# Attention with bias on one core: other engines for the first casts, another order of the first copies, one more exp bank on VectorE, other load times

## The chip, the cores and the metric

The kernel runs on one core of a Trainium2 chip. The metric is the device time of one execution in microseconds (us). The kernel before took 242.43 us (median of 3 runs, 241.94 to 243.75).

The engines are named as the profile names them: PE is TensorE (PEld its weight loads), ACT ScalarE, DVE VectorE, POOL GpSimd, SP SyncE. The last two issue most of the DMAs.

## The reference

```python
batch, n_heads, seq_len, head_dim = 4, 8, 1024, 64
scores = np.matmul(q, k.transpose(0, 1, 3, 2)) / np.sqrt(head_dim) + bias
attn = np.exp(scores - scores_max) / (np.sum(np.exp(scores - scores_max), axis=-1, keepdims=True) + 1e-8)
return np.matmul(attn, v)
```

q, k and v are float32 of shape 4 x 8 x 1024 x 64, the bias is 1 x 1 x 1024 x 1024 and the same for all 32 heads.

## The kernel before

**Pairs, passes, fills.** Two heads make a pair, so there are 16 pairs (0 to 15). The 1024 queries are cut into eight chunks of 128, and these into three passes: A (chunks 6 and 7), B (3 to 5), C (0 to 2). The pairs run in three groups: 0 to 3 through A, B, C; 4 to 8 through C, A, B; 9 to 15 through B, C, A. A step is one head of a pair in one pass. It has two fills, one of the PSUM buffer `sx` and one of `sy`, so there are 192 fills. A fill has two banks of 512 columns in pass A and three in B and C, 512 banks in all.

**Scores without reloading the bias.** Scores stay in PSUM. At a pass's start the bias is put there by matmuls (`restart` in `s_fill`, line 151). From then on each fill adds the new head's scores and subtracts the old head's in one matmul of 128 rows: the top 64 rows of KA/QA or KB/QB hold one head, the bottom 64 the other, and QA and QB carry the signs. So the next fill of a buffer waits for the exps that read it.

**Exp.** ScalarE turns the banks of a fill into weights in bf16 (`s_exp`, line 202). Of some fills the last bank is left to VectorE, which works the exp out by a polynomial in seven instructions (`d_fixed`, line 215, and the six of `d_steps`, line 220). Such a bank is called marked; a fill is marked by `mark_next` (line 586). TensorE multiplies the weights by v, with a column of ones for the sum (`av_blocks`, line 252, instruction at L265), VectorE divides (`evac`), and SP stores.

**Preparing q and k.** Loads issued by GpSimd convert to bf16 (`load_qk`, `load_v`). TensorE transposes them into the PSUM tile `px` (L140), and VectorE copies from there into KA, KB, QA, QB (`tp_done`, line 715). For pairs 0 to 3 it makes every copy itself; later, SP's DMAs make those into KB and QB.

**The prologue, lines 281 to 487, is written out by hand.** Pair 0's and pair 1's first tiles and bias chunks 6 and 7 come by SP and ScalarE queues as float32 into staging space (`sk0`, `sk0b`, `sc[6]`, `sc[7]`, `sk1`) and are cast to bf16 by ScalarE, VectorE and, for one tile, GpSimd. Seven matmuls on zeros (line 366) come first on TensorE. Then: casts of pair 0's first k, transposes (L376, L380), copies (L382 to L384), scores L393 and bias L402, the first exps (L406), cast and transposes of pair 0's second k (L428, L429, L432), its copies (L434, L435), scores of chunk 7, and so on to the first planned fill at L478.

**The rest is planned.** The loop at line 926 gives TensorE, VectorE and ScalarE their instructions in the order that a table of costs and due times makes (`EXP`, `EXP0`, `PSL`, `PSU`, `URG`, `NEAR`, `REM` and others, lines 490 to 491). Each engine then works through its own list in order. `mark_next` marks a fill when not too much of VectorE's work is still to do (`ch_left`, `REM`), and only from fill `DMIN` to fill 192 - `DTAIL`. `loads` (line 675) issues the loads of pairs 4 to 15 when so many fills have had their exps: q and k when the count is over twice the pair's first step minus `LEADK` (28), v with `LEADV` (16). Each such load waits for the exp issued last before it.

```python
            while next_load < NP and s > 2 * first_step[next_load] - LEADK and pieces[0][0] > next_load - 4:
                for x in load_qk(next_load):
                    after(x, exps[-1])
```

Of the kernel before, what the change touches and what calls it, by code (L numbers as in the profile page):

```python
# [9 lines left out]
BF = mybir.dt.bfloat16  # L10
# [6 lines left out]
def kernel(  # L17
# [202 lines left out]
    def d_steps(ch):  # L220
        y = ys[ch % 2]
        e = de.tile([P, 512], BF, name="e")
        dtiles[ch] = e
        lo = y.bitcast(U16).rearrange("p (q w) -> p q w", w=2)[:, :, 0]
        hi = y.bitcast(I16).rearrange("p (q w) -> p q w", w=2)[:, :, 1]
        v_ = nc.vector
        return [
            (350, lambda: v_.tensor_scalar(sf, lo, G / 65536.0, None, op0=ALU.mult)),  # L228
            (350, lambda: v_.tensor_scalar(sp, hi, 0.0, 128.0, op0=ALU.max, op1=ALU.mult)),  # L229
            (610, lambda: v_.scalar_tensor_tensor(sb, sf, U2, sf, op0=ALU.add, op1=ALU.mult)),  # L230
            (610, lambda: v_.scalar_tensor_tensor(y, sf, U1, sf, op0=ALU.add, op1=ALU.mult)),  # L231
            (610, lambda: v_.scalar_tensor_tensor(sb, sb, V2, sp.bitcast(BF), op0=ALU.add, op1=ALU.mult)),  # L232
            (720, lambda: v_.scalar_tensor_tensor(e[:], y, V1, sb, op0=ALU.add, op1=ALU.mult)),  # L233
        ]
# [46 lines left out]
    with tc.manual_schedule():  # L281
# [145 lines left out]
        k0b = [sk0b[:, i * 256:(i + 1) * 256].rearrange("p (c d) -> p c d", d=D) for i in range(2)]  # L427
        cast(v_, kr0[:, 1, 4:], k0b[1])  # L428
        cast(nc.scalar, kr0[:, 1, :4], k0b[0])  # L429
# [4 lines left out]
        v_.tensor_copy(KA[D:, 0, :HK], pk0f[D:, :HK])  # L434
        v_.tensor_copy(KA[D:, 0, HK:], pk0f[D:, HK:])  # L435
# [9 lines left out]
        v_.tensor_copy(btraw[:, 7, HK:], sc[7][:, HK:])  # L445
# [45 lines left out]
        DMIN, DTAIL, DMAL, RING, PSL, PSU, URG, NEAR, REM = 14, 10, 5200, 36, 100, 200, 16, 2, 4000  # L491
        LEADK, LEADV = 28, 16
# [9 lines left out]
        raw_at = {(2, 1, 0): 12500, (2, 0, 6): 12900, (3, 1, 0): 14800, (3, 0, 6): 15200, (0, 0, 0): 16300,  # L502
                  (1, 0, 0): 23000, (2, 0, 0): 24000, (3, 0, 0): 25000}
        pieces = [(2, 1, 0, 8), (2, 0, 6, 2), (3, 1, 0, 8), (3, 0, 6, 2), (0, 0, 0, 6), (1, 0, 0, 6), (2, 0, 0, 6),
# [26 lines left out]
        def fill_banks(s):  # L531

            banks = range(2) if s in pre_done else range(nbanks(steps[s // 2][0]))
            return sorted(banks, key=lambda b: read_end.get(s - 2, {}).get(b, 0)) if s - 2 in pre_slots else list(banks)
# [20 lines left out]

        def act_cost(s):
            return EXP0 * (1 if cut_of(s) is None else 2) + EXP * banks_act(s)
# [28 lines left out]
        def mark_next(s):  # L586

            nonlocal nch
            if s in pre_slots or s != len(fill_end) or not DMIN <= s < NS - DTAIL or s - 1 in mark or len(open_ch) >= 3 \
                    or len(ch_run) >= 2 or ch_left[0] > REM:  # L590
                return
            mark.add(s)
            d_of[s, nbanks(steps[s // 2][0]) - 1] = nch
            av_left[s] -= 1
            open_ch[nch] = 1
            ch_run.append(nch)
            ch_left[0] += 3850
            nch += 1
# [75 lines left out]

        def loads():

            nonlocal next_load, next_v, dma_t
            s, t = len(act_end), t_act
            while next_load < NP and s > 2 * first_step[next_load] - LEADK and pieces[0][0] > next_load - 4:
                for x in load_qk(next_load):  # L680
                    after(x, exps[-1])
                dma_t = max(dma_t, t + 2800) + 1500
                raw_at[next_load, 1, 0] = dma_t
                dma_t += 1500
                raw_at[next_load, 0, 0] = dma_t
                next_load += 1
            while next_v < NP and s > 2 * first_step[next_v] - LEADV \
                    and not any(units[u][1] == next_v - RP for u in range(av_u, NU)):
                for x in load_v(next_v):
                    after(x, exps[-1])  # L690
                dma_t = max(dma_t, t + 2800) + 2000
                v_ready[next_v] = dma_t + 1000
                next_v += 1

        def pe_piece():
# [9 lines left out]
            ready = max(free + LATE, raw_at[pr, which, c0]) + SEM  # L705
# [7 lines left out]
            return ready, cost, emit  # L713

        def tp_done(pr, which, c0, n, px, tag, t):
# [33 lines left out]
            if which:  # L749
                if pr <= 3:  # L750
                    step(c1, lambda: nc.vector.tensor_copy(KB[:D, r, cs], flat[:D]), [("KBt", pr)])
                if pr <= 2:
                    step(c1, lambda: nc.vector.tensor_copy(KB[D:, r1, cs], flat[D:]), [("KBb", pr + 1)])
                step(c1, lambda: nc.vector.tensor_copy(KA[:, r, cs], flat), [("KA", pr)], 0, free)  # L754
            else:
                if pr <= 3:
                    step(c1, lambda: nc.vector.tensor_copy(QB[:D, r, cs], flat[:D]), [("QBt", pr)])
                if pr <= 2:
                    step(c1, lambda: sc_(QB[D:, r1, cs], flat[D:], -1.0, None, op0=ALU.mult), [("QBb", pr + 1)])
                step(cq, lambda: sc_(QA[:, r, cs], flat, sgn[:, :1], None, op0=ALU.mult), [("QA", pr)], 0, free)  # L760
# [14 lines left out]

            def next_(t1):
                cost, f = todo.pop(0)

                def run(t2):
                    f(t2)  # L780
                    if todo:
                        next_(t2 + cost)
                dve_q.append((t1, 0, cost, run))
            next_(t)
# [59 lines left out]
        def pe_pick():  # L844
            s = len(fill_end)
            f = pe_fill()
            if f and f[0] <= t_pe:
# [12 lines left out]
            for kind, c in enumerate((pe_piece(), pe_pre(), pe_av())):  # L860
# [3 lines left out]
                if kind == 0 and in_a and f and f[0] <= start + 300:  # L864
# [34 lines left out]
        def act_pick():  # L899
# [20 lines left out]
            for s, a, z in todo:  # L920
                t0 = max(t, (pre_done[s] + 470 if a == 2 and s in pre_done else bank_end[s][z - 1]) + P2E)
                t = t0 + EXP0 + EXP * (z - a)
# [70 lines left out]
```

## Time and profile before

| | |
|---|---|
| runs | 241.94, 242.43, 243.75 us |
| the profiled execution | 242.75 us, span 240.8 us |
| exps of the planned part (L204) on ScalarE | 258 instructions, 125.0 + 119.4 us busy |
| banks on VectorE (L233, last step of each) | 39 |
| copies QA (L760) on VectorE | 18, 670 ns in the mean |
| v loads by GpSimd | 32, 128 KB each, 10.3 us from issue to landing (median) |
| k loads by GpSimd | 14, 256 KB each, 4.3 us |

A row of the page's groups has line, engine, operation, tile written and tile read, count, busy time, mean of one, and idle time before it. The timeline has start, length, engine, line, operation and shapes, and in brackets how long the engine was idle before and what released it. Exps that follow one another overlap in the trace by about 0.1 us, so the busy time of ScalarE counts a little more than the time that passes. TensorE's ends are modelled.

The start and the end of the planned part, in ScalarE's timeline:

```
15.26 1.02 ACT L204 ACTIVATE E<-sx 128x1024 bf16<-128x1024 f32 x1
235.91 1.08 ACT L204 ACTIVATE E<-sy 128x512 bf16<-128x512 f32 x2
```

### The profile page before, as it was taken

Reading aid. Unit: us, or ns where it says so; the run is one execution under the profiler, and the core shown is the slowest. Engines: PE = TensorE matmul, PEld = TensorE weight load, DVE = VectorE, ACT = ScalarE, POOL = GpSimd, SP = SyncE. Lnnn points to the kernel's source line nnn. Section 1 sums busy time; section 2 is a strip of 40 time slices with the busy share of each in tenths; the row PEclk is TensorE's granted clock in tenths of the full one; section 3 lists DMA queues with packets and bytes.
Section 4 is the critical chain, followed back from the end, with each engine's and each line's share of the span. In section 5 each row is a group of like instructions: output and inputs, shape, how many; then the busy total and the mean of one; then the engine's idle time right before and its main releaser. Section 6 shows DMA issues by size and latency. Waiting matters only on the chain.

```text
span 240.8 us, 9418 instructions
## 1 busy us (share of the span) xinstructions
PE 225.0 (93%) x4009; PEld 188.6 (78%) x4009; DVE 219.0 (91%) x456; ACT 226.2 (94%) x273; POOL 56.7 (24%) x80
## 2 busy tenths in 40 slices
PE   7996989999999999999999999989999899998993
PEld 3775868888877889998777787777888777797882
DVE  3576999979999999999999999979999999999992
ACT  4588999999999999999999999989999999999993
POOL 4594322255241000013365444200000000000000
PEclk9999999999999999999999999999999999999998
DMA  7899997989999522039899999994121121111112
GB/s 223 223 147 181 171 164 136 169 165 180 228 197 200 135 69 66 5 93 169 142 168 196 227 237 220 195 198 97 38 65 39 34 69 36 33 35 35 50 42 67
DMA packets 60633, 30.98 MB, mean 129 GB/s; under 512 B 36016, under 2 KB 56624, under 8 KB 60592
## 3 DMA queue, kind: packets, MB, share of 16 engines
q0 software_dynamic: 42272, 13.50, 54.2%
q1 hardware_dynamic: 18176, 16.62, 25.4%
q8 instruction: 31, 0.51, 0.9%
q10 hardware_dynamic: 144, 0.26, 0.5%
q14 instruction: 10, 0.08, 0.1%
HBM read 29.36 MB, written 8.39 MB: 157 GB/s over the span
## 4 chain that ended last, share of the span: by engine, by line
PE 57%; ACT 16%; DVE 15%; issue 7%; DMA 4%; ACTq 0%; DVEq 0%
PE po L265 18%; PE sx L176 16%; PE sy L176 15%; ACT E L204 15%; PE px L140 5%; DMA out_dram<-ob 3%; DVE scr L216 2%; DMA E<-in_k_dram 1%; DVE scr L231 1%; DVE scr L230 1%; DVE ob L277 1%; DVE QA L760 1%; DVE KA L754 1%; DVE scr L232 1%; DVE e L233 1%
## 5 line engine op out<-in xcount | busy, mean ns | idle before, releaser
L204 ACT ACTIVATE E<-sy 128x512 bf16<-128x512 f32 (+2 forms) x141 | 125.0, 941 | 0.6 <-PE sy L176 0.2
L204 ACT ACTIVATE E<-sx 128x1024 bf16<-128x1024 f32 (+2 forms) x117 | 119.4, 1049 | 3.3 <-PE sx L176 2.7
L265 PE MATMUL po<-VV,E 128*128 128x65 bf16 x1892 | 82.9, 194 | 2.3 <-DVE KA L754 0.7
L265 PEld LDWEIGHTS <-E 128*128 128x128 bf16 x1892 | 75.3, 98 | 9.9 <-issue 2.7
L176 PEld LDWEIGHTS <-KA 128*128 128x128 bf16 x648 | 47.3, 97 | 10.8 <-issue 3.1
L176 PEld LDWEIGHTS <-KB 128*128 128x128 bf16 x600 | 43.7, 98 | 13.7 <-issue 5.7
L176 PE MATMUL sx<-QB,KB 128*128 128x128 bf16 (+2 forms) x300 | 34.8, 251 | 4.8 <-ACT E L204 2.8
L176 PE MATMUL sy<-QA,KA 128*128 128x128 bf16 (+2 forms) x312 | 36.8, 251 | 0.8
L176 PE MATMUL sx<-QA,KA 128*128 128x128 bf16 (+2 forms) x312 | 35.8, 252 | 0.7 <-ACT E L204 0.2
L176 PE MATMUL sy<-QB,KB 128*128 128x128 bf16 (+2 forms) x300 | 34.9, 251 | 0.7 <-ACT E L204 0.5
L134 POOL DMA_DIRECT2D VV<-in_v_dram x32 | 28.9, 905 | 22.7 <-ACT E L204 10.8
L233 DVE SCALAR_TENSOR_TENSOR e<-scr 128x512 bf16<-128x512 f32 x39 | 26.8, 688 | 0.9
L232 DVE SCALAR_TENSOR_TENSOR scr<-scr 128x512 f32<-128x512 f32 x39 | 26.6, 683 | 0.0
L230 DVE SCALAR_TENSOR_TENSOR scr<-scr 128x512 f32<-128x512 f32 x39 | 26.6, 682 | 0.0
L231 DVE SCALAR_TENSOR_TENSOR scr<-scr 128x512 f32<-128x512 f32 x39 | 26.6, 682 | 0.0
L277 DVE TENSOR_TENSOR ob<-po,rs 128x384 f32<-128x384 f32 (+2 forms) x49 | 24.8, 506 | 1.7
L131 POOL DMA_DIRECT2D kr<-in_k_dram x12 | 8.7, 723 | 68.5 <-ACT E L204 63.9
L228 DVE TENSOR_SCALAR scr<-scr 128x512 f32<-128x512 uint16 x39 | 17.4, 447 | 0.1
L229 DVE TENSOR_SCALAR scr<-scr 128x512 int16<-128x512 int16 x39 | 17.0, 435 | 0.0
L216 DVE TENSOR_SCALAR scr<-sx 128x512 int32<-128x512 f32 x24 | 16.4, 683 | 0.2
L760 DVE TENSOR_SCALAR QA<-px,sgn 128x1024 bf16<-128x1024 bf16 (+2 forms) x18 | 12.1, 670 | 2.7 <-PE px L140 2.5
L140 PE MATMUL px<-ident,qr 128*64 128x128 bf16 x256 | 11.4, 224 | 1.1 <-issue 1.1
(81 smaller groups left out, 175.5 us busy)
## 6 DMA issues: line engine op xcount, KB each, us to landing
out_dram<-ob SPq DMA_DIRECT2D x32, 192.0 KB, 2.6
VV<-in_v_dram POOLq DMA_DIRECT2D x32, 128.0 KB, 10.3
kr<-in_k_dram POOLq DMA_DIRECT2D x14, 256.0 KB, 4.3
KB<-KA SPq DMA_DIRECT2D x24, 128.0 KB, 7.0
qr<-in_q_dram POOLq DMA_DIRECT2D x12, 256.0 KB, 6.5
QB<-qn SPq DMA_DIRECT2D x22, 128.0 KB, 7.0
out_dram<-ob SPq DMA_DIRECT2D x15, 128.0 KB, 2.3
btraw<-in_bias_dram POOLq DMA_DIRECT2D x2, 768.0 KB, 9.9
```

What stands on the lines that cost most here:

```text
L134: return [nc.gpsimd.dma_start(out=VV[:, pr % RP, t * NCH:(t + 1) * NCH, :D], in_=vf[pr][:, t].rearrange("p (c d) -> p c d", d=D)) for t in ...
L140: nc.tensor.transpose(px[t * D:(t + 1) * D, c, :], src[:, t, c0 + c, :], ident[:])
L176: m = nc.tensor.matmul(o, lhsT, rhs, start=restart and i == 0, stop=i == len(todo) - 1 or not restart, skip_group_check=True)
L204: x = nc.scalar.activation(E[:, at:at + (hi - lo) * 512], XY[s % 2][:, lo * 512:hi * 512], ACTF.Exp, scale=scale)
L216: i = nc.vector.tensor_scalar(ys[ch % 2].bitcast(I32), XY[s % 2][:, b * 512:(b + 1) * 512], scale * LOG2E * 65536.0, 127.0 * 65536.0, op0= ...
L228: (350, lambda: v_.tensor_scalar(sf, lo, G / 65536.0, None, op0=ALU.mult)),
L230: (610, lambda: v_.scalar_tensor_tensor(sb, sf, U2, sf, op0=ALU.add, op1=ALU.mult)),
L231: (610, lambda: v_.scalar_tensor_tensor(y, sf, U1, sf, op0=ALU.add, op1=ALU.mult)),
L232: (610, lambda: v_.scalar_tensor_tensor(sb, sb, V2, sp.bitcast(BF), op0=ALU.add, op1=ALU.mult)),
L233: (720, lambda: v_.scalar_tensor_tensor(e[:], y, V1, sb, op0=ALU.add, op1=ALU.mult)),
L265: nc.tensor.matmul(po[u][:, h - hs[0], c - c0, :], e_block(s, col), VV[:, pr % RP, h * NCH + kc, :], start=first, stop=left[u] == 0, skip_ ...
L277: nc.vector.tensor_tensor(ob[:], acc[:, :, :, :D], rs[:].to_broadcast([P, nh, W, D]), op=ALU.mult)
```

## The change

- **Prologue.** Eight matmuls on zeros instead of seven. Bias chunk 6's last 384 columns and chunk 7's last 512 are cast by GpSimd instead of VectorE. Pair 0's second k is cast whole by VectorE instead of by halves on VectorE and ScalarE. The copy of pair 0's second half of k stands ahead of the copy of q. Pair 3's q load stands ahead of its k load on GpSimd.
- **First copies of pairs 0 to 3.** Of a k tile, the copy into KB's top is made first; then the list waits until the first q copy of that pair is made; KA follows; the copy into the next pair's KB bottom comes last (for pairs up to 2). For q, QB's top is first, then QA, then the next pair's QB bottom. The PSUM tile is free after the last of these.
- **Loads.** A new function `gate` sets them: pairs 4 to 8 from fill 18 on, five fills apart, v twelve fills later; pairs 9 to 15 from fill 56 on, six apart, v eight later.
- **Planner.** Costs of VectorE's steps, of single-bank exps and several thresholds; marked fills are allowed up to fill 184 instead of 182. The number of banks on VectorE goes from 39 to 40.
- **Order rules.** The early fill of a pass's third bank (`pe_pre`) goes ahead of other TensorE work when it is that fill's turn; in pass A a transpose may go ahead of a fill that is up to 0.3 us away.

```diff
-            (350, lambda: v_.tensor_scalar(sf, lo, G / 65536.0, None, op0=ALU.mult)),
...
-            (720, lambda: v_.scalar_tensor_tensor(e[:], y, V1, sb, op0=ALU.add, op1=ALU.mult)),
+            (340, lambda: v_.tensor_scalar(sf, lo, G / 65536.0, None, op0=ALU.mult)),
...
+            (650, lambda: v_.scalar_tensor_tensor(e[:], y, V1, sb, op0=ALU.add, op1=ALU.mult)),
...
+        cast(g, btraw[:, 6, 5 * P:], sc[6][:, 5 * P:])
         for pr in (2, 3):
             if pr == 3:
                 cast(g, kr1[:, 1].rearrange("p c d -> p (c d)"), sk1[:, 512:])
+                load_q(pr, 6, 8)
             x = g.dma_start(out=raws[pr, 1].rearrange("p t c d -> p t (c d)"), in_=kf[pr])
             if pr == 2:
                 after(x, behind)
-            load_q(pr, 6, 8)
+            if pr == 2:
+                cast(g, btraw[:, 7, HK:], sc[7][:, HK:])
+                load_q(pr, 6, 8)
...
-        for i in range(7):
+        for i in range(8):
...
+        on(1, 2, 3, v_.tensor_copy(KA[:D, 0, HK:], pk[1][:D]))
         v_.tensor_copy(QB[:D, 0, 6 * P:], pq_[:D].rearrange("p c q -> p (c q)"))
-        on(1, 2, 3, v_.tensor_copy(KA[:D, 0, HK:], pk[1][:D]))
         nc.scalar.copy(btraw[:, 6, :5 * P], sc[6][:, :5 * P])
-        v_.tensor_copy(btraw[:, 6, 5 * P:], sc[6][:, 5 * P:])
...
-        cast(v_, kr0[:, 1, 4:], k0b[1])
-        cast(nc.scalar, kr0[:, 1, :4], k0b[0])
+        cast(v_, kr0[:, 1], sk0b.rearrange("p (c d) -> p c d", d=D))
...
-        v_.tensor_copy(btraw[:, 7, HK:], sc[7][:, HK:])
...
-        DMIN, DTAIL, DMAL, RING, PSL, PSU, URG, NEAR, REM = 14, 10, 5200, 36, 100, 200, 16, 2, 4000
-        LEADK, LEADV = 28, 16
+        DMIN, DTAIL, DMAL, RING, PSL, PSU, URG, NEAR, REM = 14, 8, 5200, 38, 60, 150, 24, 3, 5000
+        G0, G1, G2, G3, G4, G5 = 18, 5, 12, 56, 6, 8
...
+        def gate(pr, v=0):
+
+            return G0 + G1 * (pr - 4) + G2 * v if pr < 9 else G3 + G4 * (pr - 9) + G5 * v
...
-            while next_load < NP and s > 2 * first_step[next_load] - LEADK and pieces[0][0] > next_load - 4:
+            while next_load < NP and s > gate(next_load) and pieces[0][0] > next_load - 4:
...
-            while next_v < NP and s > 2 * first_step[next_v] - LEADV \
+            while next_v < NP and s > gate(next_v, 1) \
...
-            ready = max(free + LATE, raw_at[pr, which, c0]) + SEM
+            ready = max(free + (LATE if pr > 3 else 100), raw_at[pr, which, c0]) + SEM
...
             if which:
+                early = pr <= 3
+                if early:
+                    step(c1, lambda: nc.vector.tensor_copy(KB[:D, r, cs], flat[:D]), [("KBt", pr)])
+                step(c1, lambda: nc.vector.tensor_copy(KA[:, r, cs], flat), [("KA", pr)], 0, None if pr <= 2 else free)
+                if pr <= 2:
+                    step(c1, lambda: nc.vector.tensor_copy(KB[D:, r1, cs], flat[D:]), [("KBb", pr + 1)], 0, free)
+            else:
+                early = False
                 if pr <= 3:
-                    step(c1, lambda: nc.vector.tensor_copy(KB[:D, r, cs], flat[:D]), [("KBt", pr)])
+                    step(c1, lambda: nc.vector.tensor_copy(QB[:D, r, cs], flat[:D]), [("QBt", pr)], 0, lambda t2: q_first(t2))
...
+            pre = pe_pre()
+            if pre and s in pre_slots:
+                return (max(t_pe, pre[0]),) + pre[1:]
...
-                if kind == 0 and in_a and f and f[0] <= start + 300:
+                if kind == 0 and in_a and f and f[0] <= start + (300 if dist > 6 else -300):
```

More of the change, by code (lines that the diff above doesn't have):

```diff
@@ L533, in fill_banks @@
             banks = range(2) if s in pre_done else range(nbanks(steps[s // 2][0]))
-            return sorted(banks, key=lambda b: read_end.get(s - 2, {}).get(b, 0)) if s - 2 in pre_slots else list(banks)
+            return sorted(banks, key=lambda b: read_end.get(s - 2, {}).get(b, 0)) if s in pre_slots or s - 2 in pre_slots else list(banks)
         def bank_cost(s):
@@ L780, in run @@
                     f(t2)
-                    if todo:
+                    if todo and early and len(todo) == n_all - 1 and resume.get(pr) != "go":
+                        resume[pr] = next_
+                    elif todo:
                         next_(t2 + cost)
                 dve_q.append((t1, 0, cost, run))
+            n_all = len(todo)
             next_(t)
```

44 lines of the change are left out of this document (23 added, 21 removed).

## The prediction

> **What bounds the kernel now.** I read the page's busy times first, then ScalarE's timeline for its waits, then the chain of waits around the early ones, then the stretches in windows. Times are in us from the span's start.
>
> ```profile
> PE 225.0 (93%) x4009; PEld 188.6 (78%) x4009; DVE 219.0 (91%) x456; ACT 226.2 (94%) x273; POOL 56.7 (24%) x80
> ```
>
> ScalarE (ACT) is the fullest engine, with VectorE (DVE) next; its exps (L204) follow one another almost without a break from 15.26 to 236.99. An exp that follows another starts about 0.11 before the end that the trace gives for the last (three banks: 1.45 long, one each 1.33 or 1.34). Counted so, ScalarE's gaps are 6.8 in all before 20, 1.0 from 20 to 30 and about 5.6 after that. The ones that matter, in its timeline (start, length, then what was waited for):
>
> ```profile
> 11.01 1.79 ACT L406 ACTIVATE E<-sx 128x512 bf16<-128x512 f32 x3 [1.55 <-PE sx L393]
> 13.97 1.16 ACT L406 ACTIVATE E<-sy 128x512 bf16<-128x512 f32 x2 [0.69 <-PE sy L393]
> 20.30 1.02 ACT L204 ACTIVATE E<-sx 128x1024 bf16<-128x1024 f32 x1 [0.85 <-PE sx L176]
> 158.45 1.02 ACT L204 ACTIVATE E<-sx 128x1024 bf16<-128x1024 f32 x1 [0.97 <-PE sx L176]
> ```
>
> The first two belong to the prologue. Its chain of waits has these steps (start, length, what):
>
> ```profile
> 8.65 0.30 ACT kr L285
> ...
> 8.99 1.06 PE px L432 x8
> ...
> 11.71 0.44 PE sx L402 x4
> ```
>
> So the cast of half of pair 0's second k on ScalarE, queued behind two exps, holds the transposes L432. The matmuls at 11.71 need all of bias chunk 7; the page names an exp, but the last to end before them is the cast L445 on VectorE, at 10.89 + 0.68 = 11.57. The third, at 20.30, is made on VectorE's queue:
>
> ```profile
> 17.94 0.69 DVE L753 COPY KB<-px 64x1024 bf16<-64x1024 bf16 x1
> 18.65 0.69 DVE L754 COPY KA<-px 128x1024 bf16<-128x1024 bf16 x1
> 19.25 0.27 DVE L757 COPY QB<-px 64x256 bf16<-64x256 bf16 x1
> ...
> 19.58 0.62 PE L176 MATMUL sx<-QB,KB 128*128 128x128 bf16 x8 [1.28 <-DVE QB L757]
> ```
>
> Pair 2's scores want the small copy L757, and two k copies that nobody needs yet stand ahead of it. The fourth is a break in the middle of 16 transposes, which waits for nothing that the profile shows, in the stretch with the busiest DMA:
>
> ```profile
> 157.54 0.27 PE L140 MATMUL px<-ident,qr 128*64 128x128 bf16 x3 [1.10 <-issue]
> ```
>
> ```profile
> 100.00:107.00 7.00, 6.99 (x174) 6.87 (x171) 6.90 (x16) 7.00 (x15) 0.00 (x0) 1.00 0.21 63
> 152.00:157.00 5.00, 4.44 (x91) 3.58 (x90) 4.75 (x10) 5.00 (x5) 0.87 (x1) 1.00 1.69 196
> ```
>
> The last two numbers of a window are the DMA share and GB/s: 0.21 before the loads of pairs 9 to 15 (first one at 107.23), 1.69 at their end.
>
> **The change part by part.** The sum is made against the profiled execution: 242.75, of which 240.8 is the span and 1.95 lies around it. It stands 0.32 above the median of 242.43.
>
> *Eighth dummy matmul.* Seven start at 1.00 and end at 4.17 (0.427 apart); the transposes L376 start at 4.29. An eighth ends at 4.60; a matmul starts up to 0.18 before its forerunner's modelled end, so L376 moves to between 4.42 and 4.60. I take 4.42, as the matmuls around it follow so: +0.13.
>
> *Order of the first copies.* L384 now goes ahead of L383 (k's half ahead of the q copy). L376 ends at 5.35 + 0.13, L384 runs from 5.50 and occupies 0.33 (5.81 to 6.14 now), so the q copy starts at 5.83 and ends at 6.13 instead of 5.88. The scores L393 move from 5.94 to 6.18: +0.24. From there TensorE has 24 matmuls in a row (8 scores, 16 bias) at 0.107 each, to 8.75.
>
> *Bias chunk 6's cast on GpSimd.* ScalarE's part starts at 5.45 without a wait on the load, so the load is in by then. GpSimd is idle from 3.67; its cast of 512 columns took 0.60, so 384 end before 6.05. The scores, until 7.03, hide it; without them it would cost what it is late, one for one.
>
> *Pair 0's second k in one cast on VectorE.* A 128x512 cast took 0.41 there (L287). VectorE is free at about 6.7 and the data is there at 7.03 or before: done by 7.45, so L432 waits only for TensorE: 8.75 instead of 8.99, a gain of 0.24 (0.06 if the dummy costs 0.31). ScalarE loses one 0.41 cast in a stretch where it waits anyway.
>
> *Bias chunk 7's half on GpSimd.* The load is in by 8.83 (L444). GpSimd issues pair 2's k at 7.20 to 8.02, then casts 0.60, done by 9.45 at the latest. L402 then follows the scores, which end at 11.30 - 0.24 = 11.06, with the next start near 11.0: 0.65 to 0.71 ahead of 11.71. VectorE is rid of 0.60 too, so its casts L458 end by 11.1, before TensorE wants them at 11.6. From 11.71 to 14.55 TensorE has no gap over 0.1, so the whole chain moves by 0.65. Queued behind the cast on GpSimd: pair 2's q load starts 0.6 to 1.4 later, lands (4.2 from issue) by 13.7 and is used after 17; pair 3's k load goes from 10.62 to 11.34, lands (up to 5.1) by 16.5 and is used near 19. Both are covered by over 2.5; later loads keep their places.
>
> *First q copies ahead of k's rest.* With L753 and L754 (0.71 each) behind it, L757 can run at 17.94 and not 19.25, and with the 0.65, once its transposes (18.00 now, 17.35 then) are in: about 17.65. The next fill can start near 17.95, its exp after the one that ends at 18.67. So 20.30 becomes 18.67: 1.63 in all, 0.65 of it the prologue's. What was pushed back (0.71 of KB, 0.29 of QB for pair 3) has four exps of 0.95 to be done in. Late next is the first fill of the second pass at 38.03, which waited 0.25 already.
>
> *One more bank on VectorE (40 instead of 39).* ScalarE: a 1024 exp in place of a 1536 one, 1.33 - 0.90 = -0.43. VectorE: 0.60 + 0.33 + 0.34 + 4 x 0.60 = +3.67. VectorE's idle time that a better order can fill is 1.04 (before 21.26), 1.12 (24.38), 1.23 (51.03) and 1.03 (157.85). I book -0.43 and put the other end into a rival.
>
> *Loads of pairs 9 to 15.* They start at fill 57 instead of 81, six fills apart instead of four. Of the 24 fills between, 13 take 0.95 and 11 take 1.33, so the first comes some 27 earlier, near 80, in the stretch with DMA share 0.21. GpSimd has nothing else there. A load that waits for its exp holds the v loads behind it, at no cost in this queue. The traffic in 152 to 157 goes, and with it, I suppose, the break at 157.54: -1.0. The trace shows it once; the ends are 0 and -1.08. For a tie to the DMA: the queue of code blocks moved 31 pieces, 0.51 MB, and the piece at 154 held DMA engines for 1.41 (4.4% of 16 engines in 2 us) where quiet ones took 0.93.
> [...]
>
> *New costs and thresholds of the planner.* They reorder the work after 30. The trace has no row for that: no better than the 4.5 left in ScalarE's gaps there, no worse than 1.8, the spread of the runs shown (241.94 to 243.75). I take 0 and keep -1.5 to +1.5.
>
> Sum: -1.63 - 0.43 - 1.0 = -3.06, and 242.75 - 3.06 = 239.7.
>
> **The rivals.**
> *The planner closes more gaps.* A third of the 4.5 also goes: 238.2. For it: the 5.6 are many gaps of 0.2 to 0.3. Against: TensorE is full beside them.
> *The break stays.* If it isn't the DMA's, the sum is without the -1.0: 240.7. For it: the piece at 154 was over 2 us before the break; against: with less traffic TensorE's matmuls show only one such break, 0.38 at 164.94. [...]
> *The clock.* By form, a transpose L432 took 311 ns before 10 us and L456 222 ns after. If an eighth dummy brings that step ahead of 6.2, the 32 matmuls from there to L432's end take about 0.04 less each: another -1.3, 238.4. Against: TensorE was busy from 1.00 to 5.78 but for 0.12 already, and stayed slow until about 10. [...] The trace speaks more against it than for it.
> *The start is gained and lost again.* Bias, q and v loads land when they did; if the second pass waits for them (L204 at 38.03) or the prologue's steps hide one another, 1.0 to 1.6 of the 3.06 is lost and some of the break stays: 241.6.
> *VectorE becomes the bound (slower).* From 26 to 235 it has no idle time but 1.23 and 1.03. To end 3.06 earlier with 3.67 more it must find 6.73; it has 1.63 (earlier start) + 1.03 + 3.39 (other idle) = 6.05, and about 1 at the end, where its last bank (234.37) is done 2.6 before the last exp. If that 3.39 can't be filled, the end is VectorE's: 242.75 + 3.67 - 1.63 - 1.03 = 243.8, and 244.8 if the break stays too. It decides when filled plus tail time is below about 4.
>
> **How the numbers follow.** A measurement of this kernel can tell about 1% from no change: below 240.0 is faster, above 244.9 slower. The forecast has 0.44 (own range 238.9 to 240.6, most of it below 240.0: 0.33 and 0.11), more gaps closed 0.17 and the clock 0.07 (both faster), the break staying 0.07 and the start lost 0.15 (same), VectorE 0.10 (0.06 same, 0.04 slower). Faster 0.57, same 0.39, slower 0.04. The range goes from 237.8 (below both fast rivals' values) to 242.0 (past 241.6); it leaves out VectorE's case and the far ends, under 0.2 together.
>
> **What would show it.** Right: L432 near 8.75, L402's second group near 11.0, the first L204 near 14.6 instead of 15.26, no wait at its fourth successor; 40 of L233; no "issue" break of about 1 in the transposes; the first load of pair 9 between 76 and 84. Wrong: ScalarE's gaps after 30 larger than 5.6, waits on VectorE's copies or chains named before PE or ACT, VectorE's last chain after the last exp, or matmuls that are slow beyond 10 us.

## The result, and the profile after

| | before | after |
|---|---|---|
| median, lowest to highest (17 runs each) | 242.18, 240.05 to 244.30 | 240.10, 239.28 to 241.04 |
| the profiled execution, and its span | 242.75, 240.8 | 239.70, 237.8 |
| exps of the planned part (L204) | 258 | 261 |
| banks on VectorE (L233) | 39 | 40 |
| v loads, issue to landing (median) | 10.3 | 7.4 |

The ratio is 0.9925 [0.9903, 0.9948]: 0.75% less time. All ratios here leave out disturbed runs, those more than 1.5% above the fastest of the same kernel; experiment 6 had seven of them in twelve and its profile is one, so no difference in time is taken from that profile.

The page's busy times of the changed kernel, and its shares of the chain of work that ended last:

```profile
PE 224.2 (94%) x4010; PEld 187.7 (79%) x4010; DVE 220.8 (93%) x461; ACT 225.6 (95%) x275; POOL 57.5 (24%) x82
...
DVE 49%; PE 34%; ACT 7%; issue 7%; DMA 2%; ACTq 0%; DVEq 0%
```

ScalarE is still the fullest engine, with 0.6 less work, and VectorE has 1.8 more. That chain runs mostly through VectorE now; before, it was this:

```profile
PE 57%; ACT 16%; DVE 15%; issue 7%; DMA 4%; ACTq 0%; DVEq 0%
```

Experiment 12 shows what such a share is worth. ScalarE's timeline, at the places that were shown of before:

```profile
9.43 1.58 ACT L409 ACTIVATE E<-sx 128x512 bf16<-128x512 f32 x3 [0.39 <-PE sx L396]
...
13.23 1.02 ACT L204 ACTIVATE E<-sx 128x1024 bf16<-128x1024 f32 x1
...
17.36 1.04 ACT L204 ACTIVATE E<-sx 128x1024 bf16<-128x1024 f32 x1
...
154.61 1.06 ACT L204 ACTIVATE E<-sx 128x1024 bf16<-128x1024 f32 x1
155.64 1.51 ACT L204 ACTIVATE E<-sy 128x1024 bf16<-128x1024 f32 x2
157.04 1.46 ACT L204 ACTIVATE E<-sx 128x1536 bf16<-128x1536 f32 x1
```

The first planned exp starts at 13.23 instead of 15.26; pair 2's first exp at 17.36 instead of 20.30, without a wait; and there is no break near 155. Why the start is so early is seen in TensorE's timeline:

```profile
1.00 3.60 PE L371 MATMUL sy<-zeros 128*128 128x512 bf16 x8 [1.00 <-DVE warm L308]
4.53 0.64 PE L380 MATMUL sx<-ident,kr 128*64 128x128 bf16 x4
...
6.20 0.38 PE L396 MATMUL sx<-QB,KA 64*128 64x128 bf16 x4 [0.48 <-DVE QB L388]
...
7.84 0.64 PE L433 MATMUL px<-ident,kr 128*64 128x128 bf16 x8
...
9.67 0.47 PE L405 MATMUL sx<-ident,btraw 128*128 128x128 bf16 x4
```

L433 is what was L432, and L405 what was L402. The scores start at 6.20 as forecast (6.18), but eight transposes now take 0.64 where they took 1.06: TensorE came to full speed at 5.26 and not at 10.09, where the first clock records of the two traces stand. That is the rival called the clock. VectorE's first copies, in its timeline, have the new order, the small q copy (L769) ahead of KA (L763) and of the next pair's KB (L765):

```profile
15.20 0.68 DVE L762 COPY KB<-px 64x1024 bf16<-64x1024 bf16 x1
15.80 0.27 DVE L769 COPY QB<-px 64x256 bf16<-64x256 bf16 x1
16.00 0.67 DVE L763 COPY KA<-px 128x1024 bf16<-128x1024 bf16 x1
16.60 0.33 DVE L770 TENSOR_SCALAR QA<-px,sgn 128x256 bf16<-128x256 bf16 x1
16.95 0.69 DVE L765 COPY KB<-px 64x1024 bf16<-64x1024 bf16 x1
```

The same two stretches in windows (the last two numbers are the DMA share and GB/s):

```profile
100.00:107.00 7.00, 6.87 (x142) 6.21 (x140) 6.90 (x17) 6.96 (x13) 3.31 (x5) 1.00 1.51 174
152.00:157.00 5.00, 5.00 (x108) 4.39 (x105) 4.90 (x12) 5.00 (x6) 0.00 (x0) 1.00 0.13 39
```

The traffic has moved from 152 to 157 (share 1.69 before, 0.13 now) to the stretch that was quiet (0.21 before, 1.51 now). The end is new. The last work in the timeline of the changed kernel:

```profile
231.28 1.16 ACT L204 ACTIVATE E<-sy 128x512 bf16<-128x512 f32 x2
231.32 0.69 DVE L233 SCALAR_TENSOR_TENSOR e<-scr 128x512 bf16<-128x512 f32 x1
...
232.07 0.30 PE L265 MATMUL po<-VV,e 128*128 128x65 bf16 x4 [0.28 <-DVE e L233]
...
232.62 1.32 PE L265 MATMUL po<-VV,E 128*128 128x65 bf16 x32 [0.25 <-DVE ob L277]
...
234.55 0.29 DVE L277 TENSOR_TENSOR ob<-po,rs 128x128 f32<-128x128 f32 x1 [0.40 <-DMA out_dram<-ob]
```

The last exp ends at 232.44, the last copy into `ob` at 234.84: a tail of 2.40. Before it was 0.89 (the last exp ended at 236.99, the copy at 237.88). TensorE has 32 matmuls to do after the last exp. Before, it had 4:

```profile
237.04 0.30 PE L265 MATMUL po<-VV,E 128*128 128x65 bf16 x4 [0.19 <-ACT E L204]
```

Where the time came from, as the same exp's start in the two profiles, after less before (a lead is negative; in both, the exps of L204 change between `sx` and `sy` to make 192 turns, and these are compared in order):

| place | lead at its end | change there |
|---|---|---|
| start, to the first L204 | -2.03 | -2.03 |
| copies, to the fill at 20.30 | -2.94 | -0.91 |
| 20 to 147 | -2.04 | +0.90 |
| 147 to 180 | -4.70 | -2.66 |
| 180 to the last exp's start | -4.63 | +0.07 |
| last exp's end and tail, to the span's end | -3.04 | +1.59 |

Not all of this is gained or lost time. At 147 the changed kernel's ScalarE had done one bank more than before's, since VectorE gets that bank later; one turn later, at 147.94 of before, both have done as many, and the lead is 2.48. So of the +0.90 some 0.44 is the place of a bank, and as much of the -2.66.

The profiled pair differs by 3.05 and the medians by 2.08, since the profile of before was 0.57 above its median and that of after 0.40 below.

### The profile page after: what moved, and what is told of

It reads as the page before. It is cut to its first block, busy times and chain, and to the rows that moved or that the text cites. A ratio compares the mean times of both kernels' runs of the same rounds, so it can differ in the third digit from the quotient of the medians.

```text
span 237.8 us, 9441 instructions
## 1 busy us (share of the span) xinstructions
PE 224.2 (94%) x4010; PEld 187.7 (79%) x4010; DVE 220.8 (93%) x461; ACT 225.6 (95%) x275; POOL 57.5 (24%) x82
## 4 chain that ended last, share of the span: by engine, by line
DVE 49%; PE 34%; ACT 7%; issue 7%; DMA 2%; ACTq 0%; DVEq 0%
PE sx L176 9%; PE po L265 8%; PE sy L176 8%; ACT E L204 7%; DVE scr L216 7%; DVE scr L232 7%; DVE e L233 6%; DVE ob L277 6%; DVE scr L231 5%; DVE scr L230 4%; DVE scr L229 4%; PE px L140 4%; DVE scr L228 3%; DVE QA L770 2%; DVE rs L276 2%
## 5 line engine op out<-in xcount | busy, mean ns | idle before, releaser
L204 ACT ACTIVATE E<-sy 128x512 bf16<-128x512 f32 (+2 forms) x151 | 127.9, 906 | 0.2
L204 ACT ACTIVATE E<-sx 128x1024 bf16<-128x1024 f32 (+2 forms) x110 | 115.2, 1065 | 1.5 <-PE sx L176 0.9
L265 PE MATMUL po<-VV,E 128*128 128x65 bf16 x1888 | 84.2, 194 | 2.1 <-DVE ob L277 1.1
L265 PEld LDWEIGHTS <-E 128*128 128x128 bf16 x1888 | 76.0, 98 | 10.3 <-DVE ob L277 2.4
L176 PE MATMUL sx<-QB,KB 128*128 128x128 bf16 (+2 forms) x300 | 35.5, 251 | 2.4 <-ACT E L204 1.7
L176 PE MATMUL sy<-QA,KA 128*128 128x128 bf16 (+2 forms) x312 | 36.0, 252 | 0.4 <-ACT E L204 0.2
L233 DVE SCALAR_TENSOR_TENSOR e<-scr 128x512 bf16<-128x512 f32 x40 | 27.6, 690 | 1.1
L232 DVE SCALAR_TENSOR_TENSOR scr<-scr 128x512 f32<-128x512 f32 x40 | 27.4, 684 | 0.0
L230 DVE SCALAR_TENSOR_TENSOR scr<-scr 128x512 f32<-128x512 f32 x40 | 27.3, 684 | 0.0
L231 DVE SCALAR_TENSOR_TENSOR scr<-scr 128x512 f32<-128x512 f32 x40 | 27.3, 683 | 0.0
L216 DVE TENSOR_SCALAR scr<-sx 128x512 int32<-128x512 f32 x32 | 21.9, 684 | 1.7 <-ACT E L204 1.5
L176 PEld LDWEIGHTS <-btraw 128*128 128x128 bf16 x128 | 11.3, 148 | 1.2 <-issue 0.5
```

The source lines that it names most:

```text
L176: m = nc.tensor.matmul(o, lhsT, rhs, start=restart and i == 0, stop=i == len(todo) - 1 or not restart, skip_group_check=True)
L204: x = nc.scalar.activation(E[:, at:at + (hi - lo) * 512], XY[s % 2][:, lo * 512:hi * 512], ACTF.Exp, scale=scale)
L216: i = nc.vector.tensor_scalar(ys[ch % 2].bitcast(I32), XY[s % 2][:, b * 512:(b + 1) * 512], scale * LOG2E * 65536.0, 127.0 * 65536.0, op0= ...
L230: (600, lambda: v_.scalar_tensor_tensor(sb, sf, U2, sf, op0=ALU.add, op1=ALU.mult)),
L231: (600, lambda: v_.scalar_tensor_tensor(y, sf, U1, sf, op0=ALU.add, op1=ALU.mult)),
L232: (600, lambda: v_.scalar_tensor_tensor(sb, sb, V2, sp.bitcast(BF), op0=ALU.add, op1=ALU.mult)),
```

## The experiments

What was to be told apart, after this table: whether the early clock is the eighth dummy's doing; whether a lead at the start is carried to the end or lost on the way; whether the loads' times or the planner's new order gave the gain from 147 to 180; and whether the tail is the fortieth bank's and VectorE the bound there. A ratio is against the old kernel on the same chip.

**1. Before, with eight dummies.**

```diff
-        for i in range(7):
+        for i in range(8):
```

> The kernel before with eight dummy matmuls instead of seven; all else in its order. Theory 1 (the eighth dummy brings TensorE's full clock forward): matmuls near 220 ns from about 5.5 us on instead of 10, first L204 near 14.0 instead of 15.26, time lower by 0.8 to 1.3 (ratio 0.995 to 0.997). Theory 2 (the clock's step falls by chance, and the profiled execution of the changed kernel had luck): the step anywhere between 5 and 10 us, first L204 moved by +0.13 when it is late, time the same within 0.3 us (ratio 0.999 to 1.001), spread of the runs as before.

242.18, ratio 1.0022 [0.9994, 1.0051]. The first planned exp came at 13.81, 1.45 earlier, and that lead held to 147. Then the break, the pause of TensorE that waits for nothing the profile shows (`<-issue`), came back, longer:

```profile
157.07 0.30 PE L140 MATMUL px<-ident,qr 128*64 128x128 bf16 x4 [1.80 <-issue]
```

Windows of the same run (the third number from the end is the clock that TensorE was granted):

```profile
156.00:158.00 2.00, 0.93 (x11) 0.68 (x11) 0.59 (x1) 0.37 (x1) 0.00 (x0) 1.00 2.05 173
158.00:160.00 2.00, 2.00 (x22) 1.54 (x21) 1.88 (x6) 1.50 (x2) 0.00 (x0) 0.50 1.53 181
160.00:162.00 2.00, 2.00 (x29) 1.60 (x27) 1.86 (x3) 1.32 (x3) 0.00 (x0) 0.64 1.29 186
```

So a break of 1.80 was followed by half the clock (by the trace's clock records from 158.01 to 161.43), and the last exp came 0.63 later than in before. In this execution, which took 243.40, 1.2 more than the median, the break took all that the start gave. That the other executions go the same way isn't shown.

**2 and 3. Before, with the new prologue: the casts, the order of pair 0's copies and GpSimd's list, with seven dummies and with eight.** The planned part is the old one.

```diff
+        cast(g, btraw[:, 6, 5 * P:], sc[6][:, 5 * P:])
...
+                cast(g, btraw[:, 7, HK:], sc[7][:, HK:])
...
-        cast(v_, kr0[:, 1, 4:], k0b[1])
-        cast(nc.scalar, kr0[:, 1, :4], k0b[0])
+        cast(v_, kr0[:, 1], sk0b.rearrange("p (c d) -> p c d", d=D))
```

> The kernel before with the new prologue (casts moved, order of the first copies in it, pair 3's q load ahead) but seven dummies; the planned part is the same instruction for instruction. Theory 1: clock full only near 10 us, first L204 near 14.6 (my sum without the dummy's 0.13: 14.5), time lower by about 0.65 (ratio 0.997), less if the wait at pair 2's first fill swallows it. Theory 2: the same shift, with the clock's step at any place.

> The kernel before with the whole new prologue and eight dummies; the planned part is the same instruction for instruction. Theory 1: first L204 near 13.2 as in the changed kernel, and since the planned part is a row of waits on engines only, the time is lower by about 2 (ratio 0.992). Theory 2: first L204 between 13.2 and 14.6 by chance, lower by 0.65 in the median (ratio 0.997). A third view: the start is gained but lost again at loads that land when they did (bias, v): first L204 at 13.2 and the time lower by less than 0.8.

With seven: 241.75, ratio 0.9986 [0.9955, 1.0017]. TensorE's timeline:

```profile
8.80 1.06 PE L433 MATMUL px<-ident,kr 128*64 128x128 bf16 x8
11.06 0.47 PE L405 MATMUL sx<-ident,btraw 128*128 128x128 bf16 x4
...
158.08 0.27 PE L140 MATMUL px<-ident,qr 128*64 128x128 bf16 x3 [1.81 <-issue]
```

The clock stayed slow to 10 here, and the prologue alone does what the prediction's working said: 8.80 (8.75 forecast), 11.06 (near 11.0), and the first planned exp at 14.62 (near 14.6). With eight: 240.98, ratio 0.9958 [0.9935, 0.9982], first planned exp at 13.22, as in the changed kernel. Up to 20 it lacks only the copies' new order, so its pair 2 waits (ScalarE's timeline):

```profile
18.26 1.02 ACT L204 ACTIVATE E<-sx 128x1024 bf16<-128x1024 f32 x1 [0.79 <-PE sx L176]
```

18.26 against 17.36 in the changed kernel: the copies are worth 0.90 there (0.98 forecast). Both runs have the break, 1.81 and 1.45 long. It always sits in the same 16 transposes: with seven dummies 14 weight loads come ahead of it (in before and in experiment 2), with eight 13 (in experiments 1 and 3). One more matmul and weight load at the start moves it one matmul forward, so it goes with the number of instructions. Counted in the traces, each of these four breaks stands right behind the 5,313th record of TensorE (matmuls, weight loads and waits). The page has a queue of the kind `instruction`, q8, which moved 31 pieces of 16 KB (0.51 MB); it is called the code queue here. Its pieces start 255 of TensorE's records apart in the mean in before (124 to 372) and 256 in the changed kernel (135 to 372), and the only other pauses of this kind over 0.3 behind the prologue (0.38 at 164.94 in before, 0.50 at 148.60 in experiment 1) stand 257 records behind and 255 ahead of that place. From these counts alone I take the queue for TensorE's and the break for the edge of such a piece; which engine the queue serves isn't shown.

**4. After, with seven dummies.**

```diff
-        for i in range(8):
+        for i in range(7):
```

> The changed kernel with seven dummies; all else in its order. Theory 1: matmuls slow until about 10 us, first L204 near 14.6 instead of 13.23, time higher by 0.8 to 1.3 than the changed kernel (ratio to the kernel before 0.996 to 0.998 instead of 0.9925). Theory 2: the time as the changed kernel's within 0.3 us (ratio 0.992 to 0.993).

240.01, ratio 0.9929 [0.9903, 0.9956]: the changed kernel's time. The clock rose at 6.20, and the first planned exp came at 13.06. The early start met a new wait on TensorE, for a load of bias:

```profile
22.39 0.46 PE L176 MATMUL sx<-ident,btraw 128*128 128x128 bf16 x4 [0.85 <-DMA btraw<-in_bias_dram]
```

This is what is late next: apart from experiment 8 that load lands between 20.8 and 22.4 in the profiles, and the changed kernel wanted it at 21.55.

**5. After, with the last marked bank back on ScalarE** (39 banks on VectorE).

```diff
-        DMIN, DTAIL, DMAL, RING, PSL, PSU, URG, NEAR, REM = 14, 8, 5200, 38, 60, 150, 24, 3, 5000
+        DMIN, DTAIL, DMAL, RING, PSL, PSU, URG, NEAR, REM = 14, 10, 5200, 38, 60, 150, 24, 3, 5000
```

> The changed kernel with marked fills allowed only up to fill 182, as before: the 40th bank, which is the last one marked, goes back to ScalarE; the order up to there is the same. Theory A (the last bank's chain on VectorE holds the end): ScalarE's last exp ends about 0.4 later than 232.3, but the stretch from there to the end shrinks from 5.5 to about 4, so the time is lower by 0.5 to 1.2 than the changed kernel's (ratio to the kernel before 0.988 to 0.990 where the changed kernel has 0.9925). Theory B (ScalarE sets the end, the bank is worth its exp): time higher by 0.4 (ratio 0.994).

239.07, ratio 0.9868 [0.9823, 0.9913]. Its last exp starts 1.43 later than the changed kernel's, yet its span is 0.2 shorter. The end in its timeline:

```profile
232.71 1.08 ACT L204 ACTIVATE E<-sy 128x512 bf16<-128x512 f32 x2
...
233.84 0.30 PE L265 MATMUL po<-VV,E 128*128 128x65 bf16 x4 [0.19 <-ACT E L204]
...
234.39 0.29 DVE L277 TENSOR_TENSOR ob<-po,rs 128x128 f32<-128x128 f32 x1
```

Four matmuls are left after the last exp instead of 32, and the tail is 0.89 again. Of the 1.43, 0.48 was there from 65 on, long ahead of the fortieth bank; the other 0.95 comes from 222 on and is what ScalarE loses without it. So the bank saves ScalarE 0.95 and lengthens the tail by 1.51: a loss of some 0.56 in this pair of profiles. That the kernel is faster without it is likely from the times, but it isn't shown by ratios on the same chip (the changed kernel stood at 0.9925 [0.9903, 0.9948] and, on a third chip, at 0.9886 [0.9841, 0.9931]).

**6 and 7. The load times, taken out of the change and put into before.**

```diff
-            while next_load < NP and s > gate(next_load) and pieces[0][0] > next_load - 4:
+            while next_load < NP and s > 2 * first_step[next_load] - 28 and pieces[0][0] > next_load - 4:
...
-            while next_v < NP and s > gate(next_v, 1) \
+            while next_v < NP and s > 2 * first_step[next_v] - 16 \
```

Experiment 7 is the reverse of this in before, with `gate` and its numbers as in the change.

> The changed kernel with the load times of before for pairs 4 to 15 (the planner reorders part of its work for them). Theory A (the break in the transposes near 157 is a block of code that comes late behind the loads' traffic): a break of TensorE of 1 to 1.8 with no releaser comes back between 140 and 165, time higher by 1 to 1.8 than the changed kernel's (ratio 0.997 to 1.000). Theory B (the break belongs to the old order of work, not to the loads): no break over 0.4, time within 0.5 of the changed kernel's.

> The kernel before with the changed kernel's load times alone (the planner reorders part of its work for them). Theory A: the break of 1.1 to 1.8 in the transposes between 154 and 158 goes or falls below 0.4, time lower by 1 to 1.5 (ratio 0.994 to 0.996). Theory B: the break stays, time within 0.5 (ratio 0.998 to 1.002).

The change without them: ratio 1.0046 [0.9991, 1.0101], so the rest of the change shows no gain without the loads. The break is back. Since the planned order is another, it stands at another instruction (TensorE's timeline), but again right behind the 5,313th record:

```profile
156.45 1.12 PE L176 MATMUL sy<-QB,KB 128*128 128x128 bf16 x5 [2.19 <-issue]
```

Before with them alone: 239.04, ratio 0.9873 [0.9819, 0.9927], as much as the whole change or more. By the medians of that chip, 241.45 and 239.04, it is 2.4 us less. TensorE shows no wait of that kind over 0.3 in its span, and the window that held the break is quiet:

```profile
152.00:157.00 5.00, 4.98 (x96) 4.04 (x93) 4.93 (x12) 5.00 (x5) 0.00 (x0) 1.00 0.34 86
```

Against before in the profile, its exps lead by 0.30 from the start, by 1.12 at 147 and by 3.0 from 171 on. ScalarE's gaps between 130 and 180 are 1.0 there and 3.2 in before.

The code queue shows what the loads do. In the nine profiles without the break its 20th piece starts when TensorE has 5,057 to 5,114 records behind it. In the five with the break (before, experiments 1, 2, 3 and 6) it starts only at 5,248 to 5,307, in before 5.0 us after the 5,057th record. In all five, TensorE went on 1.28 to 1.45 after that piece had landed. So I read the break as TensorE waiting for a piece of code that comes late, an inference from these times alone. With the loads spread the piece starts at the lower counts and the break is gone.

**8. After, with the load of bias chunks 3 to 5 ahead of pair 0's q load,** against the wait of experiment 4.

```diff
-        load_q(0, 0, 6)
         g.dma_start(out=btraw[:, 3:6, :], in_=bf_[:, 3:6, :])
+        load_q(0, 0, 6)
```

> The changed kernel with the load of bias chunks 3 to 5 issued ahead of pair 0's q load on GpSimd; nothing else moves. With seven dummies the second pass's first bias matmuls waited 0.85 for that load. Theory A (with the earlier start this load is what comes late next in part of the runs): no wait of TensorE on btraw, spread of the runs smaller at the top, median lower by 0.1 to 0.4 (ratio 0.991 to 0.992). Theory B (the load is hidden in most runs): same within 0.2. It could cost if pair 0's q, 0.6 later and behind 768 KB, comes late for the second pass: then a wait of the transposes before 22 us.

241.55, ratio 1.0004 [0.9970, 1.0038], a loss against the change's 0.9925. Two lines of its timeline, of TensorE and of ScalarE:

```profile
20.55 0.53 PE L140 MATMUL px<-ident,qr 128*64 128x128 bf16 x12 [1.32 <-DMA qr<-in_q_dram]
...
21.44 1.08 ACT L204 ACTIVATE E<-sy 128x512 bf16<-128x512 f32 x2 [1.11 <-PE sy L176]
```

Now q is the late one, by more. At this speed of the start GpSimd's list of loads has no slack to trade between these two.

**9 and 10. Before with the new loads and the new prologue, and that with the new order of the first copies.** Both have eight dummies, 39 banks and before's planner constants.

```diff
-            while next_load < NP and s > 2 * first_step[next_load] - LEADK and pieces[0][0] > next_load - 4:
+            while next_load < NP and s > gate(next_load) and pieces[0][0] > next_load - 4:
...
+                    step(c1, lambda: nc.vector.tensor_copy(QB[:D, r, cs], flat[:D]), [("QBt", pr)], 0, lambda t2: q_first(t2))
```

The last line, with what belongs to it, is in experiment 10 alone.

> The kernel before with the new load times and the whole new prologue with eight dummies; its planned part is that of the run with the new load times alone (239.04, ratio 0.9873), instruction for instruction. Theory A (gains add where no load and no tail takes them back): first L204 near 13.2 in runs with an early clock, 14.6 otherwise, time lower than that run's by 0.65 to 1.9: 237.2 to 238.4, ratio 0.979 to 0.985. Theory B (the start is lost again at the bias load for the second pass, which lands when it did): ratio 0.986 to 0.988.

> As the run before it, and with the new order of the first copies, so that only the planner's costs, thresholds, order rules and the 40th bank are as in the kernel before. Theory A (the copies' 0.9 at pair 2's first fill adds as well): ratio 0.976 to 0.983. Theory B (with 0.9 more the second pass's bias load is late, a wait of TensorE on btraw near 22, and the reordered plan costs as much as it gains): ratio 0.982 to 0.988.

Experiment 9: 238.37, ratio 0.9826 [0.9784, 0.9868], runs from 238.13 to 239.21. It beats both kernels: the changed kernel ran at 239.81 (239.03 to 240.98) on the same chip (experiment 11). Its last exp starts 0.09 later than the changed kernel's; the gain is the tail (its timeline):

```profile
229.44 0.69 DVE L233 SCALAR_TENSOR_TENSOR e<-scr 128x512 bf16<-128x512 f32 x1
...
231.37 1.15 ACT L204 ACTIVATE E<-sy 128x512 bf16<-128x512 f32 x2
...
232.02 0.87 PE L265 MATMUL po<-VV,E 128*128 128x65 bf16 x16 [0.31 <-DVE rs L276]
...
233.12 0.29 DVE L277 TENSOR_TENSOR ob<-po,rs 128x128 f32<-128x128 f32 x1
```

The last bank on VectorE is done 2.4 ahead of the last exp's end, the last 16 matmuls start beside that exp, and the tail is 0.89.

Experiment 10: 241.12, ratio 0.9937 [0.9906, 0.9969], 2.75 slower than 9, and slower than either theory said. It leads at pair 2's first fill as forecast, but the planner, given the copies with the old constants, lays out the following work differently (ScalarE's and TensorE's lines in its timeline):

```profile
26.33 0.60 ACT L204 ACTIVATE E<-sy 128x512 bf16<-128x512 f32 x1 [1.08 <-PE sy L176]
...
29.72 1.00 PE L176 MATMUL sx<-QB,KB 128*128 128x384 bf16 x6 [0.32 <-DVE QA L766]
...
31.45 0.43 PE L265 MATMUL po<-VV,E 128*128 128x65 bf16 x8 [0.72 <-DVE QB L769]
```

Such waits for VectorE's copies cost it the lead by 80 (each exp compared with experiment 7's: -2.85 at the seventh fill, -0.8 at 40, +0.2 at 80, +1.7 at the end).

**11 and 12. After again, and after without step L231** of each bank on VectorE (its busy time falls from 220.8 to 202.8; the banks' values are then others).

```diff
-            (600, lambda: v_.scalar_tensor_tensor(y, sf, U1, sf, op0=ALU.add, op1=ALU.mult)),
+            (600, lambda: None),
```

> The changed kernel once more, as a control beside the others on the same chip: ratio 0.990 to 0.995.

> The changed kernel without one of the six steps of VectorE's polynomial (the one at L231, so the weights of the 40 banks on VectorE aren't exps): 24 us of VectorE's work gone, every other instruction in its place. Theory A (VectorE binds all through, as the chain of waits with 49% on it says): the time falls by 3 or more. Theory B (ScalarE and TensorE bind, VectorE only at the end, where its last chain comes after the last exps): the time falls by 0.5 to 1.6, all of it behind the last exp. Theory C (VectorE binds nowhere): within 0.3.

After again: 239.81, ratio 0.9886 [0.9841, 0.9931]; its exps keep within 0.16 of the first profile's, but for the stretch from 23 to 29, where they come up to 0.54 later. Without the step: 238.31, ratio 0.9826 [0.9780, 0.9871], 1.5 less. Of the 18.0 us by which VectorE's busy time fell, only 1.5 reached the end, though the page's chain gave VectorE 49%. Some of it came in the middle (0.5 by 110, 1.3 by 221), so VectorE holds the others up here and there, but it isn't the bound. The tail hardly moved (its timeline):

```profile
230.13 1.20 ACT L204 ACTIVATE E<-sy 128x512 bf16<-128x512 f32 x2
...
231.32 1.32 PE L265 MATMUL po<-VV,E 128*128 128x65 bf16 x32 [0.61 <-DVE ob L277]
...
233.24 0.29 DVE L277 TENSOR_TENSOR ob<-po,rs 128x128 f32<-128x128 f32 x1 [0.39 <-DMA out_dram<-ob]
```

The last bank was done at 230.10 here, 1.2 ahead of the last exp's end, and still 32 matmuls came after it and the tail was 2.20. So it isn't VectorE's time that makes the tail: the order of TensorE's last work is written with the fortieth bank late in it, and TensorE did it in that order here too.

## Why the prediction was right, and where it was not

The direction and the range held. The likeliest class (faster, below 240.0, 0.57) did not come: the median of 240.10 falls just on the side called same (0.39). And the profiled sum of -3.06 against -3.05 is luck, since terms were off by more than one microsecond on either side. On one chip (experiments 9, 10 and 11) the prologue and the loads gave some 4.2 (ratio 0.9826) where 0.65 + 1.0 was forecast; the copies under the old constants then cost 2.75, and the constants, the order rules and the fortieth bank gave 1.31 of that back, together +1.44 where -0.98 - 0.43 was forecast. By the prediction's own steps:

- **Eighth dummy, order of the first copies, casts: right.** The scores came at 6.20 (6.18 forecast). With the clock as it was in before, experiment 2 gave 8.80, 11.06 and 14.62 for 8.75, 11.0 and 14.6: the -0.65 holds. Gains made ahead of the first planned exp were carried one for one through the planned part, until a load or a break took them (experiment 1 to 147, experiment 2 to 138; experiment 3 lost 0.30 of its 2.04 between 55 and 60).
- **The rival called the clock: it happened, and had 0.07.** Its size was right: 2.03 - 0.65 = 1.38 for 1.3. "Against: TensorE was busy ... already" misjudged it. Every one of the ten profiles with eight dummies shows the step at 6.6 or before (four of them by the end of the dummies), and of the four with seven, three show it at about 10 and one at 6.2. So with eight dummies (3.60 in the changed kernel's trace) the step came early each time, with seven (3.17 in before) once in four, and with eight alone its moment, the first clock record, moved by 2.95 (3.64 to 6.59). What sets that moment isn't shown. Whether the step pays in the median stays open: the dummy alone moved it by +0.2, -0.8 and -0.1 (before against experiment 1, 2 against 3, 4 against after), with a break or a late load eating the lead in the profiles of the first and the last.
- **Copies: right where they are, wrong about the rest.** 0.90 for 0.98 at pair 2's fill. The copies pushed back did find their time; but of the lead that the start and the copies had made, 0.90 was gone again by 147 (0.46 when equal numbers of banks are compared), nearly all of it between 80 and 115, where experiment 9 with the old copies and constants lost nothing. That is the rival in which the start is lost again, as far as it came true.
- **Planner's constants, "I take 0 and keep -1.5 to +1.5": not 0, and tied to the copies.** With the old constants the copies cost 2.75 at the end (experiment 10). With the new ones, the order rules and the fortieth bank the time is 1.31 less again (experiment 11), and since that bank alone seems to cost some 0.56, the constants and rules gave nearer 1.9 by an estimate from these two, past the end that was kept. The whole change stands 1.4 above experiment 9 (239.81 against 238.37). A re-planned order is worth more than any of the small terms, and nothing in the trace of before could have priced it.
- **Fortieth bank, -0.43: mis-sized, with the wrong sign.** The rival named the right engine, but not the mechanism: VectorE didn't become the bound of the stretch; the bank's place in the order left 32 matmuls for the end, 1.51 longer, against 0.95 saved on ScalarE (experiments 5, 9 and 12). VectorE's last chain ended 0.43 ahead of the last exp, so the sign given ("VectorE's last chain after the last exp") didn't even show it. The page's chain, with 49% on VectorE, did look like this rival; only taking the work off (experiment 12) showed that it wasn't.
- **Loads, -1.0: the mechanism was right, the size far too small.** The first load of pair 9 came at 78.64 ("near 80"), the break went, and with it a stretch of gaps: some -2.2 in the profile from 147 to 180, and -1.27% [-1.81, -0.73] for the loads alone (experiment 7), which is 3.1 us (2.4 by the medians of that chip). I priced the one break seen, 1.10. Its length varies (1.10, 1.45, 1.80, 1.81, and 2.19 in experiment 6), and behind the one of 1.80 the granted clock was 0.50 for 3.4 (experiment 1). The profile of before showed the shortest of these. The rival in which the break stays fell: in all five profiles with the old load times the break stands behind the same count of records and ends 1.28 to 1.45 behind the landing of a late piece of code, and none of the nine with the new ones has it. In before no other such pause behind the prologue is over 0.38. What was held for that rival, a piece at 154 over 2 us ahead, was the piece's start; it had landed at 156.09, 1.45 before TensorE went on.
- **"Late next is the first fill of the second pass at 38.03": wrong, and misread.** At 38.03 stands an exp from the middle of the second pass; in before that pass begins with the bias matmuls at 24.72. What is late next is the bias load for them, which landed at 22.34 in experiment 4, and GpSimd's list can't give it room without making q late (experiment 8).

What stays open: why the changed plan gives back the other half of that lead between 80 and 115; what the new constants do without the new copies, which wasn't tried; the fortieth bank on one chip with the changed kernel; the wait of the last `ob` copy for an output transfer (0.40), which wasn't tried with another buffer.

## What to carry to other kernels

A single pause with nothing waited for is a sample, not a price: move its suspected cause by itself, and look at the spread of the runs too (before and experiments 1 to 3, with the break in their profiles, spread over 2.5 to 5.6 in sets of 12 to 30 runs, one run of 1182 left out; the kernels without it over 0.9 to 2.6 in sets of 6 to 17). In a kernel whose order is written ahead by a planner, an edit is worth what the new order is worth, so try each part in the old order first: here the loads and the prologue gave more than the whole change. Count what is left after the last instruction of the fullest engine: work taken off that engine near the end can come back behind it.

## What the runs showed of the hardware

- **TensorE stood still where a piece on the code queue came late.** It stood for 1.10 to 2.19 right behind its 5,313th record, in stretches with a DMA share of about 1.6 to 2.05, and went on 1.28 to 1.45 after the queue's 20th piece had landed (before and experiments 1, 2, 3 and 6). In before that piece took 1.39, from 154.70 to 156.09, and TensorE went on at 157.54. The changed kernel has a share of 1.51 from 100 to 107 without any such break, so that share alone didn't bring one; whether and which transfers held the piece up wasn't settled.
- **Half the clock came with a pause of 1.80, and not with one of 1.81.** In experiment 1 the pause ended at 157.07 and the granted clock was 0.50 from 158.01 to 161.43. In experiment 6 the pause of 2.19 ended at 156.45, and by its windows the clock was 0.50 from about 155.7 to 159.1. In experiment 2 the pause of 1.81 ended at 158.08 and the clock stood at 1.00 from 154 to 162, as it did in experiment 3 (pause of 1.45). TensorE's busy time decides no better: in the 3.41 ahead of the half clock it was 1.61 in experiments 1 and 6, and in the 3.41 up to the end of experiment 2's pause it was 1.60. What decides isn't shown.
- **The clock row doesn't show the slow start.** It stands at 1.00 (in tenths, 9 or more) from the first slice, while from 7.0 to 8.7 matmuls of 128 columns are issued every 0.107 in before and every 0.060 in the changed kernel (medians). The trace's first clock record comes only with the step itself (10.09 in before, 5.26 in the changed kernel), so the length of the matmuls has to be read.
